# Inverting the delta rule's diagonal blocks: 16x16 blocks on VectorE and a merge on TensorE, or whole 32x32 blocks on GpSimd

## The chip, the cores and the metric

The kernel runs on one core of one Trainium2 chip. The metric is the device time of one execution in microseconds, as the median of the runs. The core has five instruction queues that matter here: PE (TensorE, with its weight loads PEld), DVE (VectorE), ACT (ScalarE), POOL (GpSimd) and SP (SyncE, which here only issues transfers). Each queue runs its instructions in the order in which they stand; the engines meet through semaphores.

## What is computed

One inference step of a small decoder: a gated delta-rule mixer with 8 heads, a ConvFFN, an HGRN2 mixer and a second ConvFFN, for one prompt of 1024 tokens and 8 samples of 8 tokens. The change lies in the delta-rule mixer. Cut to what matters:

```python
def _gated_delta(q, k, v, beta, g, S0):          # chunks of the tokens
    A = where(strictly lower, (kb @ kc.T) * decay, 0)          # kb = beta * k
    sol = triangular_solve(A + eye, [v * beta, kb * exp(G)], unit_diagonal=True)
    # then a scan over the chunks: u = uv - w @ S;  o = qg @ S + attn @ u;  S = S * gl + kd.T @ u
```

The kernel forms the inverse X of (I + A) for each 128-token chunk: it inverts small diagonal blocks by substitution and merges them with matmuls, from 32 to 64 to 128.

## The kernel before

All matmuls are fp32 or split into high and low halves, with 128-partition tiles. The kernel is written with a framework that reorders each engine's instructions when the program is built, by its own model of their times; on the chip the order is fixed. Tiles come from pools: tiles with one tag share its buffers, and a new tile waits until all users of the old one are done.

The mixer's work is written as one generator per head, `gdn_head(h)`, in eight stages, and the loop at L1150 to L1155 interleaves head h and head h+1. For one head the stages are: (1) project k and convolve it (`conv_silu`); (2) load the decay rows `dec`, cut them to a triangle with an affine select on POOL (L784), exponentiate them on ACT (L788), multiply them into k k' (PE L796) to get Z (DVE L797), write Z to DRAM, and compute a row factor nE that goes to DRAM as `ed` (L825) and comes back as `Ep` (L837); (3) project q; (4) invert the diagonal blocks; (5) project v and the gate; (6) merge the blocks into X128; (7) the scan over the eight chunks (L987 to L1015); (8) the samples.

Stage 4 before the change: 72 blocks of 16x16 lie one to a partition. DVE computes their inverses row by row, with a product (L874) and a sum (L876) for each of rows 1 to 15, and a transposed copy (L877). They go to DRAM as `td` (L879) and come back with rows on partitions as `mg` (L880), and ACT spreads them out (L890, L891). Stage 6 before: three sets of 32x32 matmuls merge pairs of 16x16 blocks to 32x32 (PE L929, L934, L938), with DVE between them (L930, L940, L943); then 32 to 64 (L953, L959, L962) and 64 to 128 (L971, L974).

Z has the tag D1, which has one buffer, and L971 is the last step of head h that reads it. So Z of head h+1 (L797) is written after the merge of head h. In PE's order the matmuls for it (L796) stand right behind L974. The tiles `fs` and `mg` have the tags D9 and D7, with one buffer each.

POOL also issues DMAs: the history rows of the convolution (`gbuf`, L718) and its new state (L736), the writes of Z, `ed`, `td`, outputs and `ohl`. In `conv_silu` POOL also makes the small copies L720, L734 and L735.

Of the kernel before, what the change touches and what calls it, by code (L numbers as in the profile page):

```python
# [9 lines left out]
F32 = mybir.dt.float32  # L10
# [3 lines left out]
AF = mybir.ActivationFunctionType  # L14
# [5 lines left out]
NT = 1024  # L20
# [22 lines left out]
def trunk_kernel(ctx: ExitStack, tc: tile.TileContext, a: dict, o: dict):  # L43
# [664 lines left out]
    m16 = cload("m16", [128, 32])  # L708
    m16e = cload("m16e", [128, 2])
    nc.vector.tensor_scalar(gnorm, gnorm, 0.5, None, op0=ALU.mult)  # L710

    def conv_silu(p, kind, h, dst):
# [6 lines left out]
        nc.gpsimd.memset(xp[:, 0:3], 0.0)  # L719
        nc.gpsimd.tensor_copy(xs[:, :, 0:3], bf)  # L720
# [13 lines left out]
        nc.gpsimd.tensor_copy(st[:, 0:3], xp[:, NT:NT + 3])  # L734
        nc.gpsimd.tensor_copy(st[:, 3:27].rearrange("p (s t) -> p s t", t=3), xs[:, :, 8:11])  # L735
# [13 lines left out]
    def gdn_head(h):  # L749
# [59 lines left out]
        def evac_k(b, p):  # L809
# [3 lines left out]
            else:  # L813
# [11 lines left out]
        nc.gpsimd.dma_start(out=ed[par].rearrange("(t k) i -> (k i) t", k=8), in_=nE)  # L825


        fs = big("D9", [128, 1024], name="fs")
        f16 = lambda i: fs[:72, 256 * i:256 * i + 256].rearrange("p (a b) -> p a b", b=16)
        Zp, Lp = f16(0), f16(1)  # L830
        XT = fs[:72, 512:1024].rearrange("p (a i b) -> p a i b", i=2, b=16)
        Xp, Tp = XT[:, :, 0, :], XT[:, :, 1, :]
        Ep = small("Ep", [72, 16])
        nc.gpsimd.dma_start(
            out=Zp, in_=zd[par].rearrange("t x -> (t x)").rearrange("(b y) -> b y", y=2064)[:, :2048].rearrange(
                "b (j i) -> b j i", i=128)[:, :, 0:16])
        nc.gpsimd.dma_start(out=Ep, in_=ed[par])  # L837
# [40 lines left out]
        mg = big("D7", name="mg")  # L878
        nc.gpsimd.dma_start(out=td[par], in_=fs[:72, 512:1024])  # L879
        nc.gpsimd.dma_start(out=mg[:, 0:288].rearrange("p (t x) -> p t x", x=32),  # L880
                            in_=td[par].rearrange("(t k) (r x) -> (k r) t x", k=8, x=32))

        cp = mg[:, 0:288].rearrange("p (t i c) -> p t i c", i=2, c=16)
        XTc = mg[:, 288:800].rearrange("p (t i e c) -> p t i e c", i=2, e=2, c=16)
        Xs = mg[:64, 800:832]
        x32 = mg[:, 288:800].rearrange("p (t i c) -> p t i c", i=2, c=32)
        Xc, Tc = x32[:, :, 0, :], x32[:, :, 1, :]
        EM, V = [mg[:, i:i + 256].rearrange("p (t c) -> p t c", c=32) for i in (0, 832)]
        for e in range(2):
            nc.scalar.activation(XTc[:, :, :, e, :], cp[:, 0:8], AF.Copy, scale=m16e[:, e:e + 1])  # L890
            nc.scalar.activation(Xs[:, 16 * e:16 * e + 16], cp[:64, 8, 0, :], AF.Copy, scale=m16e[:64, e:e + 1])  # L891
# [33 lines left out]
        pV, pT, pX = ps("mx", name="pV"), ps("mx", name="pT"), ps("mx", name="pX")
        for t in range(8):
            for B in range(4):
                r = slice(32 * B, 32 * B + 32)
                mm(p8(pV)[r, t, :], z3[r, t, r], Tc[r, t, :], start=True, stop=True)  # L929
        nc.vector.tensor_tensor(V, p8(pV), EM, op=ALU.mult)  # L930
        for t in range(8):
            for B in range(4):
                r = slice(32 * B, 32 * B + 32)
# [582 lines left out]
```

## Time and profile before

| what | value |
|---|---|
| median of 3 runs (lowest to highest) | 3329.41 us (3329.31 to 3330.34) |
| the profiled execution's own time | 3336.92 us |
| its span, first to last instruction | 3335.1 us |
| busy: PE, PEld, DVE, ACT, POOL | 96%, 89%, 50%, 33%, 9% |
| mean granted TensorE clock | 0.972 |
| instructions on DVE and on POOL | 3819 and 647 |

The page of the profile gives shares of the whole span. The mixer's eight heads take up the stretch from about 100 to 830 us; what is said of the change has to be read there. A chain of waits follows the work that ended last back from the end. A timeline lists one engine's instructions with start, duration and, in brackets, the idle time before them and what ended it. Windows give busy time and granted clock by stretch.

### The profile page before, as it was taken

How to read it: one execution, taken by the hardware profiler on the slowest of the kernel's cores; microseconds unless marked ns; L12 is line 12 of the kernel's file. 1: busy time of each engine (PE TensorE's matmuls, PEld its weight loads, DVE VectorE, ACT ScalarE, POOL GpSimd, SP SyncE). 2: the span in 40 equal slices, each digit the busy share in tenths (PEclk: the TensorE clock that was granted, in tenths of full speed). 3: DMA queues.
4: the chain of work that ended last, by engine and by line, in shares of the span. 5: the costliest groups of instructions: out<-in, count | busy, mean ns of one | idle time of the engine just before them, and what ended most of it. 6: DMA issues, size and time to landing. Idle time of an engine off the chain costs nothing.

```text
span 3335.1 us, 61843 instructions
## 1 busy us (share of the span) xinstructions
PE 3205.5 (96%) x25521; PEld 2983.3 (89%) x25521; DVE 1669.9 (50%) x3819; ACT 1086.1 (33%) x2475; POOL 289.6 (9%) x647
## 2 busy tenths in 40 slices
PE   7899999998989999999998999999999999999997
PEld 5888888887979999999996999999888999999997
DVE  6667667774562233333437644555465233333345
ACT  4343334442342312131234333333334331222222
POOL 0211111110010000000001000000010000000002
PEclk9999999998989999999998999999999999999999
DMA  6333333224322222222213121112531111111113
GB/s 201 95 94 99 91 99 95 70 78 152 112 89 86 80 88 86 81 87 80 93 56 115 55 73 63 57 57 89 179 111 42 45 46 45 46 45 45 41 63 105
DMA packets 164634, 277.98 MB, mean 83 GB/s; under 512 B 20056, under 2 KB 91480, under 8 KB 164352
## 3 DMA queue, kind: packets, MB, share of 16 engines
q1 hardware_dynamic: 145328, 236.24, 22.6%
q0 software_dynamic: 15616, 37.15, 3.8%
q8 instruction: 201, 3.29, 0.4%
q10 hardware_dynamic: 3408, 0.63, 0.1%
q14 instruction: 81, 0.66, 0.1%
HBM read 222.48 MB, written 51.47 MB: 82 GB/s over the span
## 4 chain that ended last, share of the span: by engine, by line
PE 88%; DVE 5%; DMA 3%; issue 2%; ACT 1%; POOL 1%; ACTq 0%; SPq 0%; POOLq 0%; DVEq 0%
PE pp L113 7%; PE pp L114 7%; PE pp L115 7%; PE pg L113 5%; PE pu L113 5%; PE pg L115 5%; PE pg L114 5%; PE pu L115 5%; PE pu L114 5%; PE pd L113 5%; PE pd L115 5%; PE pd L114 5%; PE pf L113 1%; PE adap L176 1%; PE pf L115 1%
## 5 line engine op out<-in xcount | busy, mean ns | idle before, releaser
L113 PE MATMUL pp<-h,wi 128*128 128x384 f32 (+1 forms) x1536 | 524.5, 343 | 12.2 <-DVE adasb L184 8.5
L114 PE MATMUL pp<-h,wi 128*128 128x384 f32 (+1 forms) x1536 | 524.1, 342 | 0.0
L115 PE MATMUL pp<-h,wi 128*128 128x384 f32 (+1 forms) x1536 | 522.3, 340 | 0.0
L113 PE MATMUL pg<-h,wg 128*128 128x384 f32 (+1 forms) x1056 | 347.8, 330 | 0.0
L115 PE MATMUL pg<-h,wg 128*128 128x384 f32 (+1 forms) x1056 | 346.6, 328 | 0.0
L113 PE MATMUL pu<-h,wu 128*128 128x384 f32 (+1 forms) x1056 | 346.3, 328 | 0.0
L114 PE MATMUL pg<-h,wg 128*128 128x384 f32 (+1 forms) x1056 | 346.1, 328 | 0.0
L115 PE MATMUL pu<-h,wu 128*128 128x384 f32 (+1 forms) x1056 | 344.8, 327 | 0.0
L114 PE MATMUL pu<-h,wu 128*128 128x384 f32 (+1 forms) x1056 | 344.3, 326 | 0.0
L113 PEld LDWEIGHTS pp<-h,wi 128*128 128x128 f32 x1536 | 297.5, 194 | 28.1 <-DVE adasb L184 9.2
L114 PEld LDWEIGHTS pp<-h,wi 128*128 128x128 f32 x1536 | 297.8, 194 | 7.0 <-issue 1.9
L115 PEld LDWEIGHTS pp<-h,wi 128*128 128x128 f32 x1536 | 297.6, 194 | 5.6 <-issue 3.5
L113 PE MATMUL pd<-mh,wd 128*128 128x384 f32 (+1 forms) x912 | 299.6, 330 | 0.0
L115 PE MATMUL pd<-mh,wd 128*128 128x384 f32 (+1 forms) x912 | 297.4, 326 | 0.0
L114 PE MATMUL pd<-ml,wd 128*128 128x384 f32 (+1 forms) x912 | 297.1, 326 | 0.0
L113 PEld LDWEIGHTS pg<-h,wg 128*128 128x128 f32 x1056 | 200.0, 189 | 7.4 <-issue 7.4
L113 PEld LDWEIGHTS pu<-h,wu 128*128 128x128 f32 x1056 | 198.2, 188 | 7.8 <-issue 6.2
L114 PEld LDWEIGHTS pg<-h,wg 128*128 128x128 f32 x1056 | 199.8, 189 | 1.3 <-issue 1.3
L115 PEld LDWEIGHTS pg<-h,wg 128*128 128x128 f32 x1056 | 199.8, 189 | 0.0
L598 DVE TENSOR_TENSOR facc<-facc,pd 128x384 f32<-128x384 f32 (+1 forms) x192 | 97.6, 510 | 203.1 <-PE pd L115 203.1
L115 PEld LDWEIGHTS pu<-h,wu 128*128 128x128 f32 x1056 | 198.2, 188 | 0.0
L114 PEld LDWEIGHTS pu<-h,wu 128*128 128x128 f32 x1056 | 198.2, 188 | 0.0
(449 smaller groups left out, 5755.6 us busy)
## 6 DMA issues: line engine op xcount, KB each, us to landing
adaw<-in_ada_w SPq DMA_DIRECT2D x96, 512.0 KB, 3.8
wgr<-in_w_gu SPq DMA_DIRECT2D x88, 256.0 KB, 2.6
wur<-in_w_gu SPq DMA_DIRECT2D x88, 256.0 KB, 2.5
wir<-in_w_gin SPq DMA_DIRECT2D x64, 256.0 KB, 2.7
wdr<-in_w_dn SPq DMA_DIRECT2D x64, 256.0 KB, 2.6
wir<-in_w_hin SPq DMA_DIRECT2D x64, 256.0 KB, 2.6
og<-ohl SPq DMA_DIRECT2D x32, 384.0 KB, 7.0
xg<-xd SPq DMA_DIRECT2D x24, 384.0 KB, 4.9
```

The lines of the kernel that those rows point to most:

```text
L113: mm(out, wh, rh(k), start=(first and i == 0), stop=False)
L114: mm(out, wh, rl(k), start=False, stop=False)
L115: mm(out, wl, rh(k), start=False, stop=(last and i == len(ks) - 1))
L176: mm(pt[32 * q:32 * q + 32, :256], cs[:, k, :], w[:, 256 * q:256 * q + 256], start=(not held or k == 0), stop=(not held or k == 7), tile_p ...
L598: nc.vector.tensor_tensor(am, am, p[:, :n], op=ALU.add)
```

## The change

In stage 4 the blocks are now 36 of 32x32, still one to a partition. POOL does the whole inversion, column by column: for each of 31 columns it forms an outer product (L875) and adds it to the inverse (L877). Columns 3 and 4 are cut in two, which makes 33 pairs of instructions with 2 x 5456 elements per partition. Ahead of them POOL multiplies Z by `Ep` (L869, 1024 elements), behind them it makes a transposed copy (L879, 1024 elements). `td` is written by two DMAs (L881, L882) in pieces of 32 elements, and read back as `mg` by one. `ed` and `Ep` keep their way through DRAM. The three matmul sets of the 16-to-32 merge are gone from stage 6, with their DVE and ACT steps; ACT copies the 32x32 blocks into X128 (L923). The small copies of `conv_silu` move from POOL to ACT and its memset to DVE. Two small constants are no longer loaded.

```diff
@@ conv_silu @@
-        nc.gpsimd.memset(xp[:, 0:3], 0.0)
-        nc.gpsimd.tensor_copy(xs[:, :, 0:3], bf)
+        nc.vector.memset(xp[:, 0:3], 0.0)
+        nc.scalar.copy(xs[:, :, 0:3], bf)
...
-        nc.gpsimd.tensor_copy(st[:, 0:3], xp[:, NT:NT + 3])
-        nc.gpsimd.tensor_copy(st[:, 3:27].rearrange("p (s t) -> p s t", t=3), xs[:, :, 8:11])
+        nc.scalar.copy(st[:, 0:3], xp[:, NT:NT + 3])
+        nc.scalar.copy(st[:, 3:27].rearrange("p (s t) -> p s t", t=3), xs[:, :, 8:11])
@@ gdn_head, stage 4 @@
-        tc.keep_in_program_order(nc.vector.tensor_tensor(Lp, Zp.rearrange("p j i -> p i j"), Ep.unsqueeze(2).to_broadcast([72, 16, 16]), op=ALU.mult))
...
-        for i in range(1, 16):
-            pri = fs[:72, 0:i * i].rearrange("p (c j) -> p c j", j=i)
-            nc.vector.tensor_tensor(pri, Tp[:, 0:i, 0:i].rearrange("p j c -> p c j"),
-                                    Lp[:, i:i + 1, 0:i].to_broadcast([72, i, i]), op=ALU.mult)
-            nc.vector.tensor_reduce(Tp[:, i, 0:i], pri, axis=mybir.AxisListType.X, op=ALU.add)
-        nc.vector.tensor_copy(Xp, Tp.rearrange("p i c -> p c i"))
...
-        for e in range(2):
-            nc.scalar.activation(XTc[:, :, :, e, :], cp[:, 0:8], AF.Copy, scale=m16e[:, e:e + 1])
...
+        tc.keep_in_program_order(nc.gpsimd.dma_start(out=Ep, in_=ed[par]))
...
+        nc.gpsimd.memset(Tf, 0.0)
+        nc.gpsimd.memset(Tf[:, ::33], 1.0)
+        nc.gpsimd.tensor_tensor(Zs, Zs, Ep.unsqueeze(1).to_broadcast([36, 32, 32]), op=ALU.mult)
+        for j in range(31):
+            n = 31 - j
+            for i0, i1 in ([(j + 1, j + 1 + n // 2), (j + 1 + n // 2, 32)] if j in (3, 4) else [(j + 1, 32)]):
+                po_ = 992 if j < 5 else 0
+                pri = Zf[:, po_:po_ + (i1 - i0) * (j + 1)].rearrange("p (i c) -> p i c", c=j + 1)
+                nc.gpsimd.tensor_tensor(pri, Zs[:, j, i0:i1].unsqueeze(2).to_broadcast([36, i1 - i0, j + 1]),
+                                        Tp[:, j:j + 1, 0:j + 1].to_broadcast([36, i1 - i0, j + 1]), op=ALU.mult)
+                nc.gpsimd.tensor_tensor(Tp[:, i0:i1, 0:j + 1], Tp[:, i0:i1, 0:j + 1], pri, op=ALU.add)
+        Xp = Zs
+        nc.gpsimd.tensor_copy(Xp, Tp.rearrange("p i c -> p c i"))
+        td4 = td[par].rearrange("b (r m x) -> b r m x", m=2, x=32)
+        nc.gpsimd.dma_start(out=td4[:, :, 0, :], in_=Tp)
+        nc.gpsimd.dma_start(out=td4[:, :, 1, :], in_=Xp)
+        mg = big("D7", [128, 9, 2, 32], name="mg")
...
+        T32, X32, Xs = mg[:, 0:8, 0, :], mg[:, 0:8, 1, :], mg[:64, 8, 1, :]
@@ gdn_head, stage 6 @@
-                mm(p8(pV)[r, t, :], z3[r, t, r], Tc[r, t, :], start=True, stop=True)
...
-                mm(p8(pT)[r, t, :], Xc[r, t, :], V[r, t, :], start=True, stop=True)
...
-                mm(p8(pX)[r, t, :], V[r, t, :], Xc[r, t, :], start=True, stop=True)
...
-            nc.vector.tensor_tensor(X128[r, :, r], Xc[r], p8(pX)[r], op=ALU.add)
+            nc.scalar.copy(X128[r, :, r], X32[r])
```

POOL's queue before, from the fetch of `Ep` of head 1 to the affine select of head 2 (the inversion of head 1 itself is on DVE; the names are tiles, `ohl` the head's output in DRAM):

```order
L837 DMA Ep<-ed 72x16
L718 DMA gbuf<-in_gbuf 128x24
L1016 DMA out_p_gdn<-sn 128x128
L856 MEMSET gqe 128x1
L1041 DMA out_s_gdn<-S_1450 128x8x128
L660 DMA ohl_913<-oh 128x1088
L661 DMA ohl_913<-g 128x1088
L784 AFFINE_SELECT dec<-dec 128x1024
```

POOL's queue now, first at the fetch of `Ep` of head 1, where the inversion starts (`tt` is the inverse, `fs` holds Z and the products):

```order
L860 DMA Ep<-ed 36x32
L869 TENSOR_TENSOR fs<-fs,Ep 36x1024
L996 DMA out_p_gdn<-sn 128x128
L867 MEMSET tt 36x1024
L868 MEMSET tt 36x32
L875 TENSOR_TENSOR fs<-fs,tt 36x31
L877 TENSOR_TENSOR tt<-tt,fs 36x31
```

And further on in the same inversion, at the affine select of head 2:

```order
L875 TENSOR_TENSOR fs<-fs,tt 36x231
L734 DMA out_gconv<-gst 128x27
L877 TENSOR_TENSOR tt<-tt,fs 36x11x21
L875 TENSOR_TENSOR fs<-fs,tt 36x220
L782 AFFINE_SELECT dec<-dec 128x1024
L877 TENSOR_TENSOR tt<-tt,fs 36x10x22
L716 DMA gbuf<-in_gbuf 128x24
```

The affine select and the DMA issues, which stood with nothing between them, now stand among the 66 instructions of the inversion.

PE's queue before, at the merge of head 2 (the `pp` rows are the k projection of head 3; the 32 matmuls of L929 stand fourteen rows earlier):

```order
L113 MATMUL pp<-h_266,wi 128x384
L114 MATMUL pp<-h_266,wi 128x384
L934 MATMUL pT<-mg 32x32 x32
L938 MATMUL pX<-mg 32x32 x32
L115 MATMUL pp<-h_266,wi 128x384
L113 MATMUL pp<-h_266,wi 128x384
L953 MATMUL pV<-fs,Z 32x32 x16
```

Three sets of small matmuls stand among the projection's, each behind a step of DVE or ACT. PE's queue now, at the same merge (`adap` is a piece of the conditioning vectors):

```order
L114 MATMUL pp<-h_266,wi 128x384
L933 MATMUL pV<-mg,Z 32x32 x16
L115 MATMUL pp<-h_266,wi 128x384
L176 MATMUL adap<-adaw,cs 32x256
L939 MATMUL pT<-fs,X_907 32x32
L942 MATMUL pX<-X_907,fs 32x32
L939 MATMUL pT<-fs,X_907 32x32 x7
```

The first matmul that needs `mg` is now that of the 32-to-64 merge; the work that stands ahead of it is nearly the same.

## Rows read from the trace of the kernel before

**Rows 1.** The page, chain that ended last, shares of the span by engine:
```profile
PE 88%; DVE 5%; DMA 3%; issue 2%; ACT 1%; POOL 1%; ACTq 0%; SPq 0%; POOLq 0%; DVEq 0%
```

**Rows 2.** PE's waits: engine line <- releaser: us in total, times, longest:
```profile
PE pV L929 <- ACT mg L890: 22.5, 8, 5.5
```

**Rows 3.** The chain in order of time: start us, us, what (heads 1, 3, 4, 7):
```profile
180.88 1.98 PE pkk L796 x16
...
362.59 1.98 PE pkk L796 x16
...
452.69 1.98 PE pkk L796 x16
...
709.35 1.98 PE pkk L796 x16
```

**Rows 4.** The chain of 362 to 453 us, from the inversion's end to the merge:
```profile
429.02 0.34 DVE fs L877
...
433.47 4.31 DMA mg<-td
...
445.45 0.62 PE pV L953 x32
```

**Rows 5.** PE by line: out<-in xcount | busy us, mean ns | idle before <-releaser:
```profile
L929 PE MATMUL pV<-mg,Z 32*32 32x32 f32 x512 | 6.7, 205 | 22.5 <-ACT mg L890 22.5
...
L938 PE MATMUL pX<-mg 32*32 32x32 f32 x512 | 6.3, 197 | 0.0
```

**Rows 6.** Timeline of POOL, 362 to 453 us:
```profile
386.38 0.59 POOL L837 DMA_DIRECT2D Ep<-ed  x1 [10.15 <-issue]
...
411.84 1.09 POOL L784 TENSOR_SCALAR_AFFINE_SELECT dec<-dec 128x1024 f32<-128x1024 f32 x1 [6.75 <-DMA dec<-gd]
```

**Rows 7.** The chain of 100 to 200 us, head 0:
```profile
146.30 4.41 DMA Ep<-ed
```

**Rows 8.** Timelines of POOL: two dependent memsets, and two-input arithmetic:
```profile
363.02 0.33 POOL L870 MEMSET fs<- 72x256 f32 x1
363.41 0.12 POOL L871 MEMSET fs<- 72x16 f32 x1
...
887.12 5.59 POOL L366 TENSOR_TENSOR acc<-acc,xg 128x256 f32<-128x256 f32 x8 [43.01 <-DVE acc L364]
...
918.11 7.77 POOL L366 TENSOR_TENSOR acc<-acc,xg 128x384 f32<-128x384 f32 x8 [0.32 <-DVE nwss L85]
```

**Rows 9.** Timelines of POOL: a copy alone, and two instructions beside DVE's:
```profile
361.95 0.20 POOL L735 COPY gst<-gxs 128x24 f32<-128x24 f32 x1
...
131.66 2.69 POOL L720 COPY gxs<-gbuf 128x24 f32<-128x24 f32 x1 [8.59 <-DVE v L732]
...
501.80 1.09 POOL L784 TENSOR_SCALAR_AFFINE_SELECT dec<-dec 128x1024 f32<-128x1024 f32 x1 [6.49 <-DMA dec<-gd]
```

**Rows 10.** Timelines of DVE, beside the POOL rows of 131, 501 and 918 us:
```profile
132.96 1.27 DVE L738 SCALAR_TENSOR_TENSOR v<-gxp,v 128x1088 f32<-128x1088 f32 x1
...
502.12 1.31 DVE L107 TENSOR_TENSOR wi<-wir,wi 128x512 fp32r<-128x512 f32 x1
...
919.03 0.15 DVE L89 TENSOR_TENSOR nwts<-snr 64x1 f32<-64x1 f32 x1
...
919.62 0.49 DVE L90 TENSOR_TENSOR nwts<-nwts,nwxs 64x1 f32<-64x1 f32 x1
```

**Rows 11.** DVE by line, 390 to 430 us (columns as in rows 5):
```profile
L731 DVE SCALAR_TENSOR_TENSOR v<-gxp,c_gcw,v 128x1024 f32<-128x1024 f32 x3 | 3.8, 1269 | 0.0
...
L107 DVE TENSOR_TENSOR wi<-wir,wi 128x512 fp32r<-128x512 f32 x4 | 2.7, 682 | 0.8 <-ACT wi L106 0.8
...
L683 DVE TENSOR_TENSOR v<-kd_s,c_smask 64x512 f32<-64x512 f32 x1 | 0.7, 676 | 0.0
```

**Rows 12.** DMA issues: out<-in queue xcount, KB each, us to landing:
```profile
mg<-td POOLq DMA_DIRECT2D x8, 144.0 KB, 4.5
```

**Rows 13.** Windows: us, busy of PE, PEld, DVE, ACT, POOL, then PEclk, DMA share, GB/s:
```profile
440.00:444.00 4.00, 4.00 (x61) 3.56 (x61) 2.19 (x3) 1.11 (x1) 0.10 (x1) 0.57 0.01 4
```

More of the change, by code (lines that the diff above doesn't have):

```diff
@@ L824, in gdn_head @@
         nc.vector.tensor_tensor(c2, nE, col(eG), op=ALU.mult)
[L825 to L837, printed above, removed]
+        nc.gpsimd.dma_start(out=ed[par].rearrange("(t k) i -> (k i) t", k=4), in_=nE)
         yield
@@ L877, in gdn_head @@
-        nc.vector.tensor_copy(Xp, Tp.rearrange("p i c -> p c i"))
[L878 to L885, printed above, removed]
@@ L886, in gdn_head @@
-        x32 = mg[:, 288:800].rearrange("p (t i c) -> p t i c", i=2, c=32)
-        Xc, Tc = x32[:, :, 0, :], x32[:, :, 1, :]
-        EM, V = [mg[:, i:i + 256].rearrange("p (t c) -> p t c", c=32) for i in (0, 832)]
-        for e in range(2):
-            nc.scalar.activation(XTc[:, :, :, e, :], cp[:, 0:8], AF.Copy, scale=m16e[:, e:e + 1])
-            nc.scalar.activation(Xs[:, 16 * e:16 * e + 16], cp[:64, 8, 0, :], AF.Copy, scale=m16e[:64, e:e + 1])
+        fs = big("D9", name="fs")
+        Zf = fs[:36, 0:1088]
@@ new lines, in gdn_head @@
+        Zs = Zf[:, 0:1024].rearrange("p (j i) -> p j i", i=32)
+        Ep = small("Ep", [36, 32])
+        tc.keep_in_program_order(nc.gpsimd.dma_start(out=Ep, in_=ed[par]))
+        nc.gpsimd.dma_start(
+            out=Zs, in_=zd[par].rearrange("t x -> (t x)").rearrange("(b y) -> b y", y=4128)[:, :4096].rearrange(
+                "b (j i) -> b j i", i=128)[:, :, 0:32])
+        tt = big("D7", name="tt")
+        Tf = tt[:36, 0:1024]
+        Tp = Tf.rearrange("p (i c) -> p i c", c=32)
+        nc.gpsimd.memset(Tf, 0.0)
@@ new lines, in gdn_head @@
+        Xp = Zs
[4 more added lines that the diff above has]
+        mg = big("D7", [128, 9, 2, 32], name="mg")
+        nc.gpsimd.dma_start(out=mg, in_=td[par].rearrange("(t k) (r y) -> (k r) t y", k=4, y=64).rearrange(
+            "p t (m x) -> p t m x", m=2))
+        T32, X32, Xs = mg[:, 0:8, 0, :], mg[:, 0:8, 1, :], mg[:64, 8, 1, :]
@@ L921, in gdn_head @@
         nEb = nE[:, 0:8].unsqueeze(2)
-        nc.vector.tensor_tensor(EM, m16.unsqueeze(1).to_broadcast([128, 8, 32]), nEb.to_broadcast([128, 8, 32]), op=ALU.mult)
         z3 = Z[:, :NT].rearrange("p (t c) -> p t c", c=128)
         p8 = lambda p, n=32: p[:, :8 * n].rearrange("p (t c) -> p t c", c=n)
[L925 to L928, printed above, removed]
-                mm(p8(pV)[r, t, :], z3[r, t, r], Tc[r, t, :], start=True, stop=True)
[L930 to L933, printed above, removed]
-                mm(p8(pT)[r, t, :], Xc[r, t, :], V[r, t, :], start=True, stop=True)
-        for t in range(8):
-            for B in range(4):
-                r = slice(32 * B, 32 * B + 32)
-                mm(p8(pX)[r, t, :], V[r, t, :], Xc[r, t, :], start=True, stop=True)
-        T32, V2 = [fs[:, i:i + 256].rearrange("p (t c) -> p t c", c=32) for i in (0, 256)]
-        nc.vector.tensor_tensor(T32, Tc, p8(pT), op=ALU.add)
+        fs = big("D9", name="fs")
+        V2 = fs[:, 256:512].rearrange("p (t c) -> p t c", c=32)
         for B in range(4):
             r = slice(32 * B, 32 * B + 32)
-            nc.vector.tensor_tensor(X128[r, :, r], Xc[r], p8(pX)[r], op=ALU.add)
+            nc.scalar.copy(X128[r, :, r], X32[r])
         T64 = fs[:64, 512:1024].rearrange("p (t c) -> p t c", c=64)
@@ L1139, in trunk_kernel @@
     zd = drp.tile([2, 9, 16512], F32, name="zd")
-    ed = drp.tile([2, 72, 16], F32, name="ed")
-    td = drp.tile([2, 72, 512], F32, name="td")
+    ed = drp.tile([2, 36, 32], F32, name="ed")
+    td = drp.tile([2, 36, 2048], F32, name="td")
     zero = big("D7", [128, 64], name="zero")
```

6 lines of the change are left out of this document (removed).

## The prediction

> **What bounds the kernel now.** I began with the page's chain that ended last: PE has 88% of it [rows 1], so a change pays where it takes work from PE or ends a wait of PE, and it costs where it makes PE wait. Next, PE's waits by line: the longest in the mixer is that of L929, the first matmul of the 16-to-32 merge, for ACT's L890, 22.5 us over 8 heads [rows 2]. The chain in order of time gives the period of a head, from one L796 to the next: 90.1 us for head 3 (362.59 to 452.69), and (709.35 - 180.88) / 6 = 88.1 us on average over heads 1 to 6 [rows 3]. At the end of a head the chain leaves PE and runs through the inversion: L877 ends at 429.36, `mg` lands at 437.78, and only then comes the merge [rows 4]. So the inversion already ends a little too late; it is hidden but for those 22.5 us.
>
> There is a loop from head to head. Z has one buffer, and PE's order puts the next L796 behind the merge, before and after the change. Whatever lies between L796 and the end of the merge (Z, `ed` through DRAM, inversion, `td`, `mg`, merges) bounds the period from below, however much PE has to do.
>
> **What it removes.** The three sets of 512 matmuls take 6.7, 6.5 and 6.3 us [rows 5]: 19.5 us of PE. With L929 goes its wait, 22.5 us [rows 2]. From L890 to the start of L953 no step is left, so 445.45 - 437.78 = 7.7 us of latency per head goes from the loop [rows 4]. DVE loses the substitution, which has an engine of its own afterwards. The small copies of `conv_silu` are cheap on ACT, a third busy and in step with the copies around them; I cost them at nothing, and at 1 us per head if ACT were late there.
>
> **What it adds: the chain on GpSimd.** Head 3, counted from its L796 at 362.59. `Ep` is issued at 386.38 [rows 6], held by `ed`, which the change leaves as it is, and takes 4.4 us to land [rows 7]: +28.2. Then POOL:
> A two-input instruction costs 5.59 / 8 = 0.699 us with 256 elements and 7.77 / 8 = 0.971 with 384 [rows 8]: 2.13 ns per element and 0.154 us fixed. One that waits for its predecessor on POOL starts 0.06 us after it, as L871 does [rows 8]; all but one of the inversion's do. So 66 x 0.214 = 14.1 us, and 10,912 elements x 2.13 ns = 23.2 us: 37.4. L869 with 1024 elements: 2.4. The transposed copy has no row of its kind: between the affine select over 1024 elements, 1.09 [rows 6], and the two-input law, 2.3; I take 1.2, since it reads one input. That broadcast or strided reads cost more, or less, than the contiguous rows here is not shown.
> In between the order has put ten other instructions (the state's output, two memsets and a third, the sample state, two `ohl` writes, a conv state, a `gbuf` load and the affine select), none over the 1.09 of the affine select, together about 5.9. POOL alone: 2.4 + 37.4 + 1.2 + 5.9 = 46.9.
>
> **What it adds: DVE and GpSimd in each other's way.** A copy of 24 elements on POOL took 2.69 us, where one of that size alone takes 0.20 [rows 9]; meanwhile DVE went through six steps with two inputs in SBUF, the last of them L738 with 1.27 [rows 10]. The other way, L107 took 1.31 us instead of 0.68 [rows 10, 11], from 502.12, until the affine select that had begun at 501.80 was through [rows 9]. Small two-input steps beside POOL's L366 took 0.49 instead of 0.15 [rows 10], while POOL kept its pace of 0.971 [rows 8]. So the two take turns: long two-input steps of DVE are added to POOL's chain, and small ones only wait. In 390 to 430 us, where the chain will run, DVE has seven groups of long ones that stay, from L731 with 3.8 us to L683 with 0.7, together 12.3 us [rows 11]. I add all 12.3; the bounds are 0 (all in POOL's own pauses) and 19 (an estimate with half as much again, for the next k convolution and the small ones).
> The Trainium skill ("SBUF — State Buffer", "Who interferes with whom") says that the two share a port pair, that an instruction of DVE with two SBUF inputs and one of GpSimd that reads SBUF exclude each other, and that the second waits until the first is through. The rows agree, but for the copy that waited for six of DVE's in a row. [...]
>
> **The sum for a head.** The chain ends at 28.2 + 46.9 + 12.3 = 87.4. `td` is now two DMAs in short pieces, and I price each like `mg`, in short pieces too: about 1.0 until the second is issued (two issues of some 0.5, as L837's 0.59 [rows 6]), 4.5 to land, and 4.5 for `mg` [rows 12]: 10.0, where before it was 8.4 [rows 4]. From there the merges run as they did from L953 to the next L796, 452.69 - 445.45 = 7.2 [rows 3, 4]. Together 104.6 us, against 90.1 now. Heads 1 to 6: 6 x (104.6 - 88.1) = +99. Head 7 has no affine select, one load less and less work of DVE beside it: about 101 against the average 88.1, +13. Head 0 has little beside it: `Ep` lands at 150.7 [rows 7], POOL takes 2.4 + 37.4 + 1.2 + 1.1, DVE adds some 6, the DMAs 10.0, the merge 7.2: 216 against 180.88 [rows 3], +35. PE's order has no more work than before to put into these waits. Sum: +147 us. The profiled execution took 3336.92 us, 7.5 more than the median of the runs; the same step on the median gives 3329.4 + 147 = 3476.
>
> The affine select now stands behind two thirds of the inversion; ACT's exponentials wait for it, behind them the second half of the weights for the next k, and behind that PE. By the sum it runs at about 436 instead of 411.84 [rows 6], which still leaves the k convolution ready before `mg` lands. That is the next in line, not an addition.
>
> The granted clock fell to 0.57 in 440 to 444 us, behind the wait and the thin matmuls of L929 [rows 13]: most of that stretch at 1.2 GHz instead of 2.4. I add nothing, since the dip is there today. The Trainium skill ("TensorE: Matmul & The Clock Gate", "HAM oscillation — how this bites in real kernels") has the array start slowly after each long wait. By that each head restarts at 1.2 GHz, and with 4.0 x 0.43 = 1.7 us lost in such a stretch the sum would be 8 x 1.7 = 14 us higher, 3490.
>
> **Rivals.** *No contention.* Should GpSimd find its turns in DVE's pauses, 7 x 12.3 + 6 = 92 us fall out: 3384. For it: POOL's pace at 918 us did not suffer. Against it: 2.69 us for a copy, and long DVE steps, not short ones.
> *Hidden, and faster.* If POOL's chain is so quick that PE reaches the merge first, only the removals count: 3329.4 - 22.5 - 19.5 = 3287. The point is the length of POOL's chain after `Ep`: up to 90.1 - 28.2 - 10.0 - 7.2 = 44.7 us head 3 stays at 90.1, and from 5 us less, 39.5, PE alone sets it (90.1 - 22.5 / 8 - 19.5 / 8 = 84.9). For it: 46.9 without contention is not far from 44.7, and the inversion may start at 390.8, as soon as `Ep` lands. Against it: the 12.3, and that 0.154 or 0.06 would have to vanish.
> *Worse.* Short strided pieces cost more than 2.13 ns per element, DVE's 19 us count in full, the late affine select pushes k behind `mg`, and the clock dips: +10 per head, 3556.
>
> **How the numbers follow.** The sum: 0.55. No contention: 0.18. Hidden: 0.12. Worse: 0.12. The last 0.03 is a tie. A measurement of this kernel tells 0.2%, 6.7 us, from no change. Faster 0.12, same 0.03, slower 0.85. The range has the sum, the rival without contention and half of the worse one: 3370 to 3570. It leaves out the faster case.
>
> **What would show it.** Right: in the new profile PE's longest wait is at the matmul behind `mg` (L933), 10 to 20 us per head, the heads' period is near 105 us, two-input steps of DVE between 390 and 450 us are longer than today, and POOL is busy for over half of a head. Wrong: L933 does not wait; the 66 instructions take well under 35 us; DVE's steps keep their length; or PE waits for the k convolution instead of `mg`.

## The result and the profile of the changed kernel

The changed kernel takes 3528.2 us (3524.6 to 3541.5, four runs) where the kernel before took 3329.4: the ratio is 1.0607, with an interval of 1.0578 to 1.0636. The forecast was 3476, in a range of 3370 to 3570. So the direction and the mechanism held, and the size came out at +199 us instead of +147. The profiled executions differ by nearly as much: their spans are 3527.4 and 3335.1 us, +192.

The chain that ended last, on the page, now has GpSimd in it (before, [rows 1]):

```profile
PE 74%; POOL 11%; DMA 5%; issue 4%; DVE 2%; ACT 1%; POOLq 0%; ACTq 0%; DVEq 0%
```

PE's waits (engine, line <- what it waited for: us in total, times, longest), against 22.5 us at L929 before [rows 2]:

```profile
PE pV L933 <- DMA mg<-td: 106.0, 8, 41.0
PE pp L113 <- DVE g L909: 32.8, 3, 18.9
...
PE pp L113 <- ACT k L726: 27.1, 3, 14.8
PE pv L764 <- DVE v L736: 18.7, 2, 17.9
PE adap L198 <- ACT k L726: 10.1, 1, 10.1
```

The longest is where it was forecast, at the first matmul that needs `mg`; together the five come to 194.7 us. The four below L933 are a second wait in each of heads 1 to 6, of 10 to 19 us, earlier in the head.

The chain in order of time (start, us, what) gives the heads' periods, as [rows 3] did, and for head 2 the four parts of which the sum was made:

```profile
224.27 3.39 PE pkk L794 x16
...
337.19 1.98 PE pkk L794 x16
...
361.12 4.06 DMA Ep<-ed
365.31 2.37 POOL fs L869
...
419.23 2.00 POOL fs L879
421.23 6.57 DMA td<-tt
...
429.26 4.05 DMA mg<-td
433.36 1.06 PE pV L933 x32
...
440.41 1.90 PE pV L951 x16
...
446.10 3.40 PE pkk L794 x16
...
896.40 1.79 PE pkk L794 x16
```

Head 1 begins 224.27 - 180.88 = 43.4 us later than before (forecast: 35). Heads 1 to 6 take (896.40 - 224.27) / 6 = 112.0 us each instead of 88.1 (forecast: 104.6), together +143.6. What is left of the 192, some 5, is head 7 and what follows (forecast: 13). The four parts, read for heads 1 to 6 as here for head 2:

| part of the loop | forecast, us | head 2 | mean of heads 1 to 6 |
|---|---|---|---|
| pkk to the first step on GpSimd (L869) | 28.2 | 28.1 | 30.4 |
| L869 to the end of L879 | 59.2 | 55.9 | 54.8 |
| end of L879 to L933 | 10.0 | 12.1 | 11.7 |
| L933 to the next pkk | 7.2 | 12.7 | 15.1 |
| period | 104.6 | 108.9 | 112.0 |

So GpSimd's share was set a little too high, and the last part, from the first merge matmul to the next pkk, at half of what it takes. Why is in the windows (us, busy time of PE, PEld, DVE, ACT, POOL with the number of instructions, granted clock, DMA share, GB/s): first the changed kernel from L933 of head 2 to the next pkk, then the kernel before from L953 to the next L796:

```profile
433.00:446.00 13.00, 12.64 (x130) 9.35 (x130) 3.85 (x6) 5.18 (x12) 0.00 (x0) 0.50 0.14 43
```

```profile
445.40:452.60 7.20, 7.20 (x130) 6.42 (x129) 3.46 (x7) 1.98 (x5) 0.00 (x0) 1.00 0.12 39
```

The same number of instructions keeps PE busy for 12.64 us at a granted clock of 0.50 and for 7.20 at 1.00. After its wait for `mg` PE does the whole merge at 1.2 GHz. Over the same part of heads 0 to 7 the granted clock is 0.50 to 0.60, behind waits of 4.3 to 41 us.

The contention of DVE and GpSimd can be read step by step. From POOL's and DVE's timelines of the changed kernel:

```profile
264.47 0.31 POOL L875 TENSOR_TENSOR fs<-fs,tt 36x56 f32<-36x56 f32 x1
264.85 1.20 POOL L877 TENSOR_TENSOR tt<-tt,fs 36x56 f32<-36x56 f32 x1
...
283.26 0.61 POOL L875 TENSOR_TENSOR fs<-fs,tt 36x255 f32<-36x255 f32 x1
283.95 0.67 POOL L877 TENSOR_TENSOR tt<-tt,fs 36x255 f32<-36x255 f32 x1
```

```profile
264.67 1.23 DVE L645 TENSOR_TENSOR ot<-ot,frs 128x1024 f32<-128x1024 f32 x1
```

A step of 56 elements takes 1.20 us beside L645, whose two inputs lie in SBUF, and 255 elements take 0.67 where DVE does nothing. The 255 steps of the eight inversions beside which DVE did nothing follow 0.175 us + 1.73 ns per element (L875) and 0.177 + 2.00 (L877), close to the forecast's 0.154 + 2.13. Held against these two lines, the 528 steps together are 62.0 us over: 61.5 of it in the 191 steps beside a DVE instruction with two inputs in SBUF, 0.6 in the 82 steps beside other work of DVE only (mostly instructions that read one of two inputs from PSUM), and none in those alone, from which the lines come. That is 7.8 us per head, where the forecast had added 12.3.

The late affine select shows in ACT's and POOL's timelines of head 1:

```profile
295.22 1.08 POOL L782 TENSOR_SCALAR_AFFINE_SELECT dec<-dec 128x1024 f32<-128x1024 f32 x1
```

```profile
296.33 0.99 ACT L786 ACTIVATE dec<-dec,nG 128x128 f32<-128x128 f32 x3 [15.33 <-POOL dec L782]
297.23 0.47 ACT L722 ACTIVATE gxp<-pp 128x384 f32<-128x384 f32 x1
```

ACT stands for 15.33 us at the exponentials, and behind them stands the evacuation of the k projection from PSUM (L722), which PE needs to go on. That is the second wait. Whether it costs anything was the first question for the experiments.

### The profile page after: what moved, and what is told of

Same layout as the page of the kernel before. It is cut to its first block, busy times and chain, and to the rows that moved or that the text cites. A ratio compares the mean times of both kernels' runs of the same rounds, so it can differ in the third digit from the quotient of the medians.

```text
span 3527.4 us, 58988 instructions
## 1 busy us (share of the span) xinstructions
PE 3229.8 (92%) x23985; PEld 2998.4 (85%) x23985; DVE 1622.0 (46%) x3531; ACT 1096.0 (31%) x2547; POOL 639.5 (18%) x1103
## 4 chain that ended last, share of the span: by engine, by line
PE 74%; POOL 11%; DMA 5%; issue 4%; DVE 2%; ACT 1%; POOLq 0%; ACTq 0%; DVEq 0%
PE pg L113 5%; PE pu L113 5%; PE pg L114 5%; PE pg L115 5%; PE pu L115 5%; PE pu L114 5%; PE pp L114 5%; PE pp L115 5%; PE pp L113 5%; PE pd L113 4%; POOL tt L877 4%; PE pd L115 4%; PE pd L114 4%; POOL fs L875 4%; DMA ed<-gc 1%
## 5 line engine op out<-in xcount | busy, mean ns | idle before, releaser
L113 PE MATMUL pp<-h,wi 128*128 128x384 f32 (+1 forms) x1536 | 532.1, 348 | 65.3 <-DVE g L909 32.8
L115 PE MATMUL pp<-h,wi 128*128 128x384 f32 (+1 forms) x1536 | 529.4, 345 | 0.0
L114 PE MATMUL pp<-h,wi 128*128 128x384 f32 (+1 forms) x1536 | 529.2, 345 | 0.1
L113 PEld LDWEIGHTS pp<-h,wi 128*128 128x128 f32 x1536 | 302.0, 197 | 84.6 <-DVE g L909 34.2
L113 PE MATMUL pg<-h,wg 128*128 128x384 f32 (+1 forms) x1056 | 347.6, 330 | 0.0
L113 PE MATMUL pu<-h,wu 128*128 128x384 f32 (+1 forms) x1056 | 346.3, 328 | 0.0
L114 PEld LDWEIGHTS pp<-h,wi 128*128 128x128 f32 x1536 | 302.7, 197 | 7.9 <-issue 2.1
L115 PEld LDWEIGHTS pp<-h,wi 128*128 128x128 f32 x1536 | 302.3, 197 | 5.6 <-issue 3.5
L113 PE MATMUL pd<-mh,wd 128*128 128x384 f32 (+1 forms) x912 | 299.6, 330 | 0.0
L537 POOL COPY fst<-fxp 128x2 f32<-128x2 f32 x44 | 8.5, 193 | 1168.4 <-ACT fxp L525 1168.4
L113 PEld LDWEIGHTS pg<-h,wg 128*128 128x128 f32 x1056 | 199.9, 189 | 6.8 <-issue 6.2
L113 PEld LDWEIGHTS pu<-h,wu 128*128 128x128 f32 x1056 | 198.2, 188 | 7.8 <-issue 6.2
```

The lines of the kernel that those rows point to most:

```text
L113: mm(out, wh, rh(k), start=(first and i == 0), stop=False)
L114: mm(out, wh, rl(k), start=False, stop=False)
L115: mm(out, wl, rh(k), start=False, stop=(last and i == len(ks) - 1))
L537: nc.gpsimd.tensor_copy(st[:, 0:2], xp[:, NT:NT + 2])
```

## Experiments on the changed kernel

Each ratio is taken against the kernel before in the same session, where its median was 3324 to 3330 us; between sessions a few microseconds say nothing.

### Does the late select cost, and does the clock?

**mask_dve** takes the select out of GpSimd's queue:

```diff
-        nc.gpsimd.affine_select(out=d3, in_=d3, pattern=[[0, 8], [1, 128]], compare_op=ALU.is_ge, fill=-1e30, ...)
+        nc.vector.tensor_tensor(d3, d3, tmask.unsqueeze(1).to_broadcast([128, 8, 128]), op=ALU.add)
```

> The changed kernel with the affine select of the decay rows (POOL, among the inversion's instructions) replaced by the addition of a constant mask on DVE. In the changed kernel PE waits a second time in heads 1 to 6, 10 to 19 us each and some 87 us in all, until shortly after the affine select. Theory 1 (one loop per head through the inversion): these waits lie in time that PE would else spend waiting for mg; with the select gone PE's waiting moves to L933, and only the 1.1 us in POOL's chain and the late k of heads 4 to 6 (some 11 us) fall out: 3505 to 3528. Rival (the late select is a cost of its own): the 87 us go, 3441.

Measured: 3527.3 us, ratio 1.0593 (1.0567 to 1.062), the same as the changed kernel. PE's waits, with L936 in the place of L933:

```profile
PE pV L936 <- DMA mg<-td: 191.2, 8, 39.9
```

The four earlier waits are gone, and L936 has taken over their time: 191.2 us against 194.7 before. The loop sets how long PE waits in a head; the select only decided where. The rival falls.

**fill32** tries to keep PE busy while it waits:

```diff
+        for t in range(32):
+            tc.keep_in_program_order(mm(pV[:, 0:128], ones, ones, start=True, stop=True))
         for t in range(8):
             for B in range(2):
...
                 mm(p8(pV)[s, t, :], z3[f, t, s], T32[f, t, :], start=True, stop=True)
```

> The changed kernel with 32 matmuls of 128x128 on constants put into PE's queue directly ahead of the first matmul that needs mg (L933); their results are overwritten. Theory 1 (loop and clock): a head's period is the loop from pkk to pkk, and its last part, from mg to the next pkk, takes 15.1 us on average instead of 7.2 because PE comes out of the wait at 1.2 GHz. The fill (about 8 us at full clock) keeps the clock up, that part falls to 8 to 10 us in heads 1 to 7, less up to 4 us in the two heads whose wait was under 5 us: about 3528 - 40 = 3488, although PE has 66 us more work. Rival (the merge is long for another reason, such as the late k): the part stays at 15 and the fill does not help: 3528 to 3560.

Measured: 3559.2 us, ratio 1.069 (1.0669 to 1.0712). The time is a miss for theory 1, and the step that it was made for is shown in some heads only. The windows of fill32 from the first merge matmul (now L935) to the next pkk, heads 1 to 5:

```profile
308.00:318.00 10.00, 9.67 (x124) 8.48 (x124) 1.54 (x3) 3.51 (x9) 0.00 (x0) 0.60 0.01 3
428.70:435.40 6.70, 6.43 (x126) 5.55 (x124) 2.89 (x5) 1.09 (x3) 0.00 (x0) 1.00 0.01 2
549.00:555.50 6.50, 6.50 (x126) 5.62 (x125) 1.54 (x3) 1.09 (x3) 0.00 (x0) 1.00 0.01 3
664.00:672.80 8.80, 8.21 (x125) 7.10 (x124) 2.90 (x5) 1.24 (x4) 0.00 (x0) 0.75 0.01 2
787.40:793.80 6.40, 6.40 (x126) 5.60 (x125) 2.37 (x5) 1.09 (x3) 0.00 (x0) 1.00 0.01 3
```

In heads 2, 3 and 5 some 126 instructions take 6.4 us at full clock, where 130 took 12.64 at half clock. But in heads 2 to 6 the fill came too late: PE still stood at the late select (`pv L764 <- DVE v L736` 86.5 us, `pp L113 <- DVE g L909` 45.8), came out of it when `mg` was almost there, and then had its projection and 7.4 us of fill to do first. In head 2 `mg` landed at 415.8 and L935 started at 428.75. Only in head 1 did the fill lie in the wait, with 3.1 us of waiting left behind it, and there the clock was 0.60 in the merge: the part took 9.8 us instead of 14.0. That head took 99.7 us (218.48 to 318.22 in the chain) instead of 112.9, but two thirds of the gain lie ahead of the merge (5.3 us before L869, 4.8 on GpSimd).

**mask_fill** puts both together, with 92 matmuls ahead of the merge.

```diff
-        nc.gpsimd.affine_select(out=d3, ...)
+        nc.vector.tensor_tensor(d3, d3, tmask.unsqueeze(1).to_broadcast([128, 8, 128]), op=ALU.add)
...
+        for t in range(92):
+            tc.keep_in_program_order(mm(pV[:, 0:128], ones, ones, start=True, stop=True))
```

> The kernel with the mask on DVE in place of the late affine select (3527), and in it 92 matmuls of 128x128 on constants ahead of L936, the first matmul that needs mg; their results are overwritten. In that kernel all of PE's waiting stands at L936, 17 to 24 us per head, and the fill is as long, about 21 us. Theory (loop and clock): the part from mg to the next pkk took 6.5 us instead of 15 in the run with 32 matmuls wherever PE came to it at full clock; here that holds for all heads and nothing else is held up, so 8 x 6 = 48 us go, and the time is about 3480, although PE gets 170 us more work. Rival (the clock is not what makes that part long, or the fill holds up the rest): 3527 or more.

Measured: 3636.4 us, ratio 1.0932 (1.0909 to 1.0956): a clear miss. ACT's timeline of head 1 tells why:

```profile
316.69 1.64 ACT L926 COPY X<-mg 32x256 f32<-32x256 f32 x4 [26.58 <-DMA mg<-td]
318.34 0.82 ACT L931 COPY fs<-mg 32x256 f32<-32x256 f32 x2
319.18 0.38 ACT L726 ACTIVATE gxp<-pp 128x256 f32<-128x256 f32 x1
```

The framework orders each engine by its own times, and with 21 us of fill on PE it put ACT's copies of `mg` ahead of the evacuation of the next k. ACT waited 26.58 us for `mg`, PE waited for ACT, and the fill (21.66 us) ran after `mg` had landed. In heads 1 to 4 it was so, and the part behind the fill took 6.3 to 6.4 us. In heads 5 and 6 the fill did lie in the wait, and the part took 23 us at a granted clock of 0.58 and 0.56, since the next k and DVE's step L941 came late there (waits of 3.2 and 9.0 us in head 5). So the clock's part in the length of the merge is shown (12.6 against 6.4 us for nearly the same instructions); that a fill would bring back its time is not.

### Is it the length of the inversion?

**short16** and **short8** leave out columns:

```diff
-        for j in range(31):
+        for j in range(16):        # short8: range(8)
```

> The changed kernel with only the first 16 of the 31 columns of the inversion (the others are left out, so what comes out is not the inverse). By GpSimd's pace in the trace of the changed kernel (0.236 us per step with its gap, 3.73 ns per element of a pair) the chain is 36.0 - 19.2 = 16.8 us shorter. Theory (the loop through the inversion sets a head's period): the time falls one for one, 8 x 16.8 = 134 us, to about 3394; if the clock recovers as well, 3350. Rival (the late select, or the new order of the work on PE, is the bound): less than half of it, 3460 or more.

> As the run with 16 columns, with only the first 8: the chain is 27.7 us shorter than in the changed kernel. Theory: 112.0 - 27.7 = 84.3 us per head, and less when the clock no longer falls, lies at the 85 us that PE's own work needs; the loop is hidden and only the removals are left: 3290 to 3310, faster than the kernel before. Rival (something else of the change costs, such as the order or the conv copies on ACT): it stays above 3330 although the inversion is short.

Measured: 3406.7 us for 16 columns, ratio 1.0242 (1.0217 to 1.0268), and 3353.6 for 8, ratio 1.0081 (1.0057 to 1.0105). The first is 121.5 us under the changed kernel where 134 were expected. The chain of short16 at the start of heads 5 to 7, and the longest of PE's waits in heads 2 to 6:

```profile
588.28 1.80 PE pkk L794 x16
683.33 1.79 PE pkk L794 x16
778.07 1.80 PE pkk L794 x16
```

```profile
PE pp L113 <- DVE g L909: 35.9, 5, 8.8
```

Over heads 1 to 6 the period is 95.9 us, 16.1 under 112.0. The part on GpSimd (L869 to the end of L879) fell by more, from 54.8 us to 35.5, and 5.0 us came back between L879 and L933. In heads 2 to 6 `mg` landed 3 to 7 us before PE came to it: PE had stood for 6 to 9 us in each at the projection, behind ACT, which waited 10 to 12 us for the late select. So the length of the inversion carries most of the loss, but not one for one: with 16 columns the select already comes last in five heads.

With 8 columns the loop no longer binds (`mg` lands 7 to 19 us before PE comes to it in heads 1 to 6), but the time stays above the kernel before and some 44 to 64 us above the 3290 to 3310 that were expected. There the expectation failed. PE's waits of short8 have the names of those behind the late select:

```profile
PE pv L764 <- DVE v L736: 15.5, 4, 5.2
PE pp L113 <- DVE g L909: 9.7, 2, 5.8
PE adap L198 <- ACT k L726: 8.0, 1, 8.0
```

Only a part of them is the select's. Ahead of L909 ACT had stood at the select for 3.1 and 6.0 us. Ahead of the waits at L764 DVE had stood for up to 6.3 us at L784, which adds a mask to `dec`, until the load of `dec` had landed (26.8 us, 6 times; the same step, L786 there, waits 0.8 in the kernel before). Ahead of the 8.0 us ACT had stood for 12.9 us at its copy of `mg` (L923). So with the short chain steps that wait for a DMA stand too early in the queues of ACT and DVE.

**mask_short8** has 8 columns and the mask on DVE.

```diff
-        nc.gpsimd.affine_select(out=d3, ...)
+        nc.vector.tensor_tensor(d3, d3, tmask.unsqueeze(1).to_broadcast([128, 8, 128]), op=ALU.add)
...
-        for j in range(31):
+        for j in range(8):
```

> Eight of the 31 columns (the others are left out) and the mask on DVE in place of the affine select. With eight columns alone 3354 was measured, some 50 above what the removals give: the chain is hidden there, but the select still stands behind the fetch of mg in POOL's queue, and PE waits 4 to 8 us per head for the next k, with the clock down behind it. Theory (the place of the select is the second cost of the change, covered as long as the chain is longer): with the select gone these waits go too, 3290 to 3315, faster than the kernel before. Rival (another part of the change costs, such as the order of PE or the work that went to ACT): 3345 or more.

Measured: 3340.4 us, ratio 1.0045 (1.0028 to 1.0062). By the ratios some 12 us (2 to 22) went with the select, so it does cost once the chain is short; the rest did not. PE still waits for v and g, and DVE for the load of `dec`: 6.9 and 6.7 us in heads 4 and 6, with 6.4 and 6.1 us of PE's waiting right behind. That points to the new order of the whole program; no run here changes that order alone, and what it costs stays open.

### Is it GpSimd?

**inv_dve** runs the same inversion on DVE:

```diff
-        nc.gpsimd.tensor_tensor(Zs, Zs, Ep.unsqueeze(1).to_broadcast([36, 32, 32]), op=ALU.mult)
+        nc.vector.tensor_tensor(Zs, Zs, Ep.unsqueeze(1).to_broadcast([36, 32, 32]), op=ALU.mult)
...
-                nc.gpsimd.tensor_tensor(Tp[:, i0:i1, 0:j + 1], Tp[:, i0:i1, 0:j + 1], pri, op=ALU.add)
+                nc.vector.tensor_tensor(Tp[:, i0:i1, 0:j + 1], Tp[:, i0:i1, 0:j + 1], pri, op=ALU.add)
```

> The changed kernel with the same inversion, instruction by instruction, on DVE instead of POOL (scaling by Ep, two memsets, 66 two-input steps and the copy). Theory 1: GpSimd's pace is the cause. On DVE 10,912 elements at 1.25 to 1.33 ns and 66 steps with some 0.12 fixed take about 22 us, 25 with the rest, some 20 to 30 less than on POOL, so mg lands before PE reaches the merge and only the removals count: about 3290, and 3330 if DVE's other work stands between the steps. Rival (the long chain of dependent steps is what costs, wherever it runs, and on DVE it holds up the convolutions too): 3420 or more.

Measured: 3555.3 us, ratio 1.0681 (1.0657 to 1.0705), slower than with GpSimd. DVE's timeline of head 2, and DVE by line in 355 to 428 us of the same head:

```profile
355.58 1.22 DVE L869 TENSOR_TENSOR fs<-fs,Ep 36x1024 f32<-36x1024 f32 x1 [6.78 <-DMA Ep<-ed]
...
366.78 0.91 DVE L867 MEMSET tt<- 36x1024 f32 x1 [0.47 <-PE pus L1012]
...
370.12 0.17 DVE L875 TENSOR_TENSOR fs<-fs,tt 36x31 f32<-36x31 f32 x1
...
426.52 0.18 DVE L877 TENSOR_TENSOR tt<-tt,fs 36x31 f32<-36x31 f32 x1
```

```profile
L877 DVE TENSOR_TENSOR tt<-tt,fs 36x31 f32<-36x31 f32 (+18 forms) x33 | 11.4, 345 | 0.4
L875 DVE TENSOR_TENSOR fs<-fs,tt 36x31 f32<-36x31 f32 (+18 forms) x33 | 10.5, 317 | 0.4
```

The 66 steps are as quick as was expected, 21.9 us. But between the first and the last of them lie 56.6 us, since DVE's queue has its other work between them, and the first stands 14.5 us behind L869: steps of the previous head's scan lie between, and the clearing of `tt` comes only behind L1012, the last reader of the previous head's `mg`, which shares the buffer. DVE in turn holds up the scan while it stands at `Ep` (PE waits 59.0 us at L979 for DVE's `ru`). The engine's pace was the wrong thing to look at; what its queue holds between the steps counts as much.

This run also shows what the merge alone takes at half clock. PE's queue holds nothing but the merge's own 112 matmuls between L933 and the next pkk here, and that part takes 8.0 us in each of heads 1 to 6, at a granted clock of 0.50.

**taps_one** asks whether it is two-input work of DVE that slows GpSimd:

```diff
-            nc.vector.scalar_tensor_tensor(dst[:, :NT], xp[:, j:j + NT], w[:, j:j + 1], dst[:, :NT], op0=ALU.mult, op1=ALU.add)
+            nc.vector.tensor_scalar(dst[:, :NT], xp[:, j:j + NT], w[:, j:j + 1], None, op0=ALU.mult)
```

> The changed kernel with the three long taps of each convolution (L729, two inputs in SBUF, 1.27 us each) made one-input steps (the accumulation is left out). In the changed kernel the 66 steps of an inversion are busy for 37.7 to 41.0 us, where their pace beside nothing gives 32 to 33; the rest is 5 to 8 us of waiting for DVE. Theory (a two-input step of DVE and one of GpSimd shut each other out): the taps are 3 of about 8 long steps beside a chain, so 2.5 to 4 us per head fall out, POOL's steps beside the one-input taps keep their pace, and by the loop the time falls 20 to 30, to about 3503. Rival (GpSimd is slowed by any work of DVE, or by memory at large): the busy time stays at 39 to 41, and the time at 3520 or more.

Measured: 3514.2 us, ratio 1.0576 (1.0547 to 1.0605), from two runs. That is 14 us under the changed kernel, or some 10 by the ratios, whose intervals overlap: the time alone settles nothing, and the busy times have to. POOL by line over the eight heads, in the changed kernel and in taps_one:

```profile
L877 POOL TENSOR_TENSOR tt<-tt,fs 36x31 f32<-36x31 f32 (+18 forms) x264 | 166.6, 631 | 19.5
L875 POOL TENSOR_TENSOR fs<-fs,tt 36x31 f32<-36x31 f32 (+18 forms) x264 | 151.3, 573 | 18.8
```

```profile
L877 POOL TENSOR_TENSOR tt<-tt,fs 36x31 f32<-36x31 f32 (+18 forms) x264 | 158.8, 602 | 19.6
L875 POOL TENSOR_TENSOR fs<-fs,tt 36x31 f32<-36x31 f32 (+18 forms) x264 | 147.2, 558 | 18.6
```

The steps lose 11.9 us of busy time, 1.5 per head, where 2.5 to 4 were expected. The direction is right, the size is not, and one step of the theory is wrong: beside a one-input tap GpSimd did not keep its pace. Steps beside L729 alone were 0.61 us over in the changed kernel (13 steps) and 0.22 over here (17 steps).

**conv_pool** undoes one part of the change:

```diff
-        nc.scalar.copy(xs[:, :, 0:3], bf)
+        nc.gpsimd.tensor_copy(xs[:, :, 0:3], bf)
...
-        nc.scalar.copy(st[:, 0:3], xp[:, NT:NT + 3])
+        nc.gpsimd.tensor_copy(st[:, 0:3], xp[:, NT:NT + 3])
```

> The changed kernel with the small copies of conv_silu and their memset back on POOL. Theory: on ACT they cost nothing, and on POOL they now stand among the inversion's steps, so that each convolution waits for its turn there: some 2 to 5 us per head later, 3530 to 3570. Rival: the move is without effect, 3528 within 7 us.

Measured: 3526.0 us, ratio 1.0593 (1.0565 to 1.0621). No difference to the changed kernel that stands out of the noise: the copies are free on either engine, and the loss comes from the rest of the change.

## Experiments on the kernel before

**b_fill** asks whether the clock behind L929 can be had back there:

```diff
+        for t in range(12):
+            tc.keep_in_program_order(mm(pV[:, 0:128], ones, ones, start=True, stop=True))
         for t in range(8):
             for B in range(4):
...
                 mm(p8(pV)[r, t, :], z3[r, t, r], Tc[r, t, :], start=True, stop=True)
```

> The kernel before with 12 matmuls of 128x128 on constants (about 2.8 us) ahead of L929, where PE waits 1.3 to 5.5 us per head. Theory (a wait of PE costs its length and then some 3.4 us at half clock): the clock stays up, some 8 x 1.7 = 14 us are gained and the fill lies in the wait: about 3316. Rival (PE has no time to give, the fill adds itself): 3335 to 3350.

Measured: 3340.4 us, ratio 1.0041 (1.0028 to 1.0054). PE's wait there fell from 22.5 us to 13.9, in four heads, but the fill (8 x 2.8 us) cost more than it gave. The 3.4 us of the theory are the time at half clock that gives 0.57 in the 4.0 us of [rows 13]. Where PE is the bound, work put into a short wait is work added.

**pool16** keeps the 16x16 blocks and the merges, and only moves the substitution to GpSimd, by columns:

```diff
+        nc.gpsimd.tensor_tensor(Lp, Zp, Ep.unsqueeze(1).to_broadcast([72, 16, 16]), op=ALU.mult)
...
+        for j in range(15):
+            n = 15 - j
+            pri = fs[:72, 0:n * (j + 1)].rearrange("p (i c) -> p i c", c=j + 1)
+            nc.gpsimd.tensor_tensor(pri, Lp[:, j, j + 1:16].unsqueeze(2).to_broadcast([72, n, j + 1]),
+                                    Tp[:, j:j + 1, 0:j + 1].to_broadcast([72, n, j + 1]), op=ALU.mult)
+            nc.gpsimd.tensor_tensor(Tp[:, j + 1:16, 0:j + 1], Tp[:, j + 1:16, 0:j + 1], pri, op=ALU.add)
```

> The kernel before, with its 16x16 blocks and merges on TensorE, and only the substitution moved: 15 columns in 30 steps on GpSimd in place of the rows on DVE. By the pace of the changed kernel's steps the chain takes 30 x 0.236 + 680 x 3.73 ns = 9.6 us, 11 to 15 with its ends and DVE's turns. In the kernel before the inversion ends 38.6 us after Ep has landed (head 3), since its first step stands 17 us behind in DVE's queue. Theory (what counts is the length of the loop, not the engine): mg lands some 20 us earlier, PE's waits at the merge (22.5 us) and the low clock behind them go, 3295 to 3315, faster than the kernel before. Rival (PE's work bounds it, or the waits go elsewhere): 3325 to 3335.

Measured: 3410.9 us, ratio 1.0266 (1.0244 to 1.0287): slower, though the chain took 12 us and `mg` was there some 40 us before PE came to the merge. PE's longest wait, then ACT and DVE in head 2 (L891 spreads `mg`, L923 is the small product):

```profile
PE pot L650 <- DVE ot L645: 79.7, 7, 15.6
```

```profile
331.73 0.51 ACT L891 ACTIVATE mg<-mg,c_m16e 128x256 f32<-128x256 f32 x1 [15.74 <-DMA mg<-td]
```

```profile
332.86 0.43 DVE L923 TENSOR_TENSOR mg<-c_m,gc 128x256 f32<-128x256 f32 x1 [14.46 <-ACT mg L891]
```

The framework had put these two steps sooner, ahead of the evacuation of v on ACT and of the previous head's output on DVE, presumably because by its own times the shorter chain is done sooner. They waited for `mg`, and all that stood behind them waited with them.

**pool16_late** moves only these steps back in their queues:

```diff
-        for e in range(2):
-            nc.scalar.activation(XTc[:, :, :, e, :], cp[:, 0:8], AF.Copy, scale=m16e[:, e:e + 1])
...
+        for e in range(2):
+            tc.keep_in_program_order(nc.scalar.activation(XTc[:, :, :, e, :], cp[:, 0:8], AF.Copy, scale=m16e[:, e:e + 1]))
...
+        tc.keep_in_program_order(nc.vector.tensor_tensor(EM, m16.unsqueeze(1).to_broadcast([128, 8, 32]), ...))
```

> As the run with the 16x16 substitution in columns on GpSimd (3411, ratio 1.027), but the steps that wait for mg, the four ACT steps that spread it out and the small product on DVE, are held back in their engines' queues until the merge, behind the next head's k. In that run the chain took 12 us and mg landed some 40 us before PE came to the merge, yet PE waited 11 to 16 us per head: ACT stood at the spreading of mg for 15 us, with the evacuation of v behind it, DVE behind ACT, and PE behind DVE. Theory (it is the place of the waiting steps in the in-order queues): PE's waits and the low clock behind them go, and the time is 3295 to 3320, under the kernel before. Rival (GpSimd's share of the work disturbs DVE and so PE in any case): 3340 or more.

Measured: 3374.2 us, ratio 1.014 (1.012 to 1.016). By the ratios about half of the loss came back, and most of the waits at L650 with it (79.7 us before, 2.8 now); ACT's wait for `mg` fell from 119.4 us to 17.5. It is still slower than the kernel before. What waits now are k and v (`pv L766 <- DVE v L738` 16.0 us, `pqk L848 <- DVE g L652` 12.6), and GpSimd and DVE hold each other up: in head 5 POOL's 30 steps are busy for 16.3 us, twice their 8.5 beside little work of DVE (head 3 of pool16). POOL by line there, 595 to 621 us:

```profile
L877 POOL TENSOR_TENSOR fs<-fs 72x15 f32<-72x15 f32 (+7 forms) x15 | 8.3, 551 | 1.1
L875 POOL TENSOR_TENSOR fs<-fs 72x15 f32<-72x15 f32 (+7 forms) x15 | 8.0, 532 | 1.1
```

How much of the remaining 45 us is contention and how much the order was not taken apart. No version here beats the kernel before.

## Why the forecast held, and where it was short

- **The loop.** That the time from pkk through the inversion to the next pkk sets a head's period was the base of the sum. short16 bears it out in the main (16.1 us of period for 19.3 us less on GpSimd, with the select coming last in five heads), and so does mask_dve: PE's waiting in a head keeps its length wherever it is put.
- **GpSimd's pace.** 37.4 us had been taken from rows of another line [rows 8]. By its own rows, 5456 x (1.73 + 2.00) ns + 33 x (0.175 + 0.177) + 66 x 0.07 us for the gaps comes to 36.6. The copy L879 takes 2.0 instead of 1.2: the bound of the two-input law was nearer than that of the affine select, although it has one input.
- **Contention.** The mechanism is shown (61.5 of 62.0 us; 82 steps beside other work of DVE lost 0.6), the term was too large: 7.8 per head in the steps instead of 12.3. Why not the whole of each DVE step is added was not taken apart; that a blocked step often begins when DVE's is partly through (L645 above had 0.18 us behind it), and that DVE also waits, would do it. The Trainium skill's rule ("SBUF — State Buffer", "Who interferes with whom"), that the two exclude each other for a whole instruction, agrees with the 1.20 us beside L645; the same section says that a DVE instruction with at most one input in SBUF does not contend outside the modes that use both port pairs, and the 0.6 us agree.
- **The late select** was called next in line, not an addition. PE did wait for it, 10 to 19 us in each of six heads, which reads like a large cost on the page. mask_dve shows that it was none: 3527 with and without. Only under a shorter chain does it cost (some 12 us, mask_short8).
- **The merge and the clock** is the step that failed. "From there the merges run as they did", 7.2 us, and for the clock "I add nothing, since the dip is there today". But before, PE waited 1.3 to 5.5 us and the dip had gone, for the most part, when L953 came; now the whole merge lies in it. From the landing of `mg` to the next pkk it is 15.1 us now and was 14.9 before (437.78 to 452.69 [rows 3, 4]), although one merge step and 7.7 us went out of it. The clock is not all of it: the merge alone takes 8.0 us at half clock (inv_dve), and the other 7 are matmuls of the projection, of `adap` and of the scan that PE's queue holds among the merge's and behind them, mostly at half clock too; 1.9 of the 7 lie between the merge's end and the next pkk, all in heads 4 to 6. Whether they could run in the wait ahead of L933 no run tries. 15.1 instead of 7.2 makes 7.9 us per head. Six heads at 7.9 and head 0 at 5 (12.2 us from L933 to the next pkk) are 52 us, and the profiled executions missed the forecast by 45. That these are close is partly luck: the other three parts of a head nearly cancel (2.2 and 1.7 us more, 4.4 less on GpSimd), and so do head 0's start (43.4 instead of 35) and the end (5 instead of 13). The Trainium skill's section on the clock ("TensorE: Matmul & The Clock Gate", "HAM oscillation — how this bites in real kernels"), by which the array restarts slowly after each long wait, pointed the right way; the price that the prediction put on it, 1.7 us per head, was that of the old dip and not of the work that would lie in the new one. The length of the wait alone does not tell the price: in head 4 the clock was 0.50 over all 16.0 us of busy PE behind a wait of 4.7 us at L933 (654.6 to 670.6); behind the 18.9 us earlier in that head, where the projection followed alone, it was 0.50 until 640 us and 0.98 in 640 to 645.
- **The parts of little weight** held: the copies on ACT cost nothing (conv_pool), and the fetches of `td` and `mg` took 11.7 instead of 10.0.
- **Rivals.** *No contention* and *hidden* are out. Of *worse*, the dip of the clock came; the late k came as a wait without a price, and steps dearer than the law did not come.

## What to carry to other kernels

When a step on a loop through several engines becomes longer, price each later step of the loop at the state in which it will find its engine: here PE did the whole merge behind its wait at half clock (0.50 to 0.60), with all that its queue held among the merge's matmuls, and that part of the loop took double. A long wait of an engine is not yet a cost: move it or shorten what it waits for, and see whether the time follows or the wait turns up elsewhere. Where a program orders each queue by its own estimate of times, shortening one step also moves those that wait for it, and an early wait at the head of an in-order queue can cost more than the step that was saved (pool16).

## What was not expected of the hardware

- A DVE instruction with one SBUF input slowed GpSimd as well: the 1024 elements of L729 as a product with a scalar took 0.75 us instead of 1.27, and GpSimd's steps beside it were still 0.22 us over. The Trainium skill ("SBUF — State Buffer", "Who interferes with whom") names this: a `tensor_scalar` can run in a mode that takes both port pairs; the trace agrees.
- A dependent step on GpSimd started 0.07 us after the one before it, and the transposed copy of 1024 elements took 1.9 to 2.1 us, nearly the two-input price.
